# Layer 0's last output projection: first chunk started on channel blocks 4 to 7, weights in half tiles, row buffers moved

## The chip, the cores and the metric

The kernel runs on one core of a Trainium2 chip. The metric is the device time in microseconds. Three runs of the kernel before gave 1709.65, 1710.34 and 1711.06 us; the median is 1710.34 us. One further execution was profiled; its own time was 1717.02 us, its span 1715.2 us.

## What is computed

The program is one step of a two-layer decoder trunk, for a prompt of 1024 tokens and 8 single-token samples, laid side by side as 1032 columns. Layer 0 is an even layer:

```
z_a, xbc, dt, glu_in, z_b = split(x @ w_in)
y   = ssd_scan(silu(conv(xbc)), dt)                    # branch a, a state-space scan
y_a = rms_norm_per_half(y * silu(z_a)) * norm_g        # the gating
y_b = silu(layer_norm(conv(glu(glu_in)))) * silu(z_b)  # branch b, a convolution branch
out = concat(y_a, y_b) @ w_out
x1  = layer_norm(ALPHA * x + out)
```

Layer 1 is sparse attention over x1. The change is in the last step of layer 0: the half of `@ w_out` that belongs to y_a.

## The kernel before, in words

Channels lie on the 128 partitions, in blocks of 128 (eight blocks make the 1024 channels), and the 1032 columns are worked in three chunks of 344 (`CH`). A float32 product is made of three matmuls of float32r halves: an operand is split into hi (a cast on ACT) and lo (a subtraction on DVE or POOL), and `mm3` (L125) adds hi*hi, hi*lo and lo*hi for each of eight channel blocks `kt`: 24 matmuls for each output block m and chunk.

The output projection has two parts. `out_b` (L728) projects the b branch block by block: weights by `load_w` into the rotating weight buffers of `wpool` (tags wst, whi, wlo, three each, half tiles of 128x512), the sum ALPHA*x + p evicted by DVE (L737) and stored to the DRAM tensor `dpart` (L738). Between these blocks the program asks for six gatings (L743). `gate(g, t0, n)` (L702) works on four channel blocks and one chunk: it loads z (L707), multiplies (L708), squares on ACT (L709), adds (L711), sums over the channels with one matmul into the PSUM buffer `pm` (L714), takes the rsqrt with two ACT functions, Ln and Exp (L174 and L175), and scales (L718). Its rows come from the pool `gz`, seven buffers of 128x344.

After `out_b` the pools `ssd`, `gz` and `ob` are closed, and the pools `wst0`, `parts0` and `outp0` are opened in the space they leave. `halves` (L754) splits the gated channels into hi and lo (L756, L757): blocks 4 to 7 over all columns first, then blocks 0 to 3 chunk by chunk. The eight weight tiles of the a branch, 128x1024 each, are loaded whole into two buffers (L775), cast on ACT (L776) and subtracted on DVE for even m and on POOL for odd m (L777), into the sixteen buffers `act` that held y_b. Then, for each chunk, the rows of `dpart` are loaded in two parts of four channel blocks (L786, four buffers of 128x4x344), the eight output blocks are made by `mm3` into PSUM (`pp`, two buffers, for even m; `pt`, five buffers, for odd m) and added to the rows (L791). `layer_norm` (L800) sums the rows (L805), takes the mean with two matmuls (L807 and L808; the second one needs block 7), subtracts it (L812), squares (L814), sums the squares (L816 or L818 and L822), takes Ln and Exp, scales (L828), makes the halves for layer 1 (L829, L830), adds the bias on POOL (L831), and stores the rows to DRAM in two parts (L793). Only that store gives a row buffer free for a later chunk.

Engines run their own instructions in order. The order on each engine is set by a planner that walks the program with a timing model: of the instructions that are ready it takes the one that stands first in the program. So head work of the scan, `out_b`, gatings, weight loads and even layer 1's first weights (L105, L142) are interleaved. `tc.issue_after(ins)` puts the instructions of its block behind `ins` on the engine of `ins`, and binds nothing on other engines. Pools on the left side are laid one after the other in the order in which they are opened. A tile that lands on bytes of a closed pool waits for the last use of those bytes.

Of the kernel before, what the change touches and what calls it, by code (L numbers as in the profile page):

```python
# [9 lines left out]
F32 = mybir.dt.float32  # L10
F32R = mybir.dt.float32r
I32 = mybir.dt.int32
AF = mybir.ActivationFunctionType
ALU = mybir.AluOpType
# [4 lines left out]
T = 1032  # L19
NP = 1024  # L20
NS = 8
CH = [(0, 344), (344, 344), (688, 344)]
# [22 lines left out]
GLU_V, GLU_G, XBC, ZA, ZB, OA, OB = 0, 8, 16, 28, 36, 44, 52  # L45
# [39 lines left out]
def psum(k, shape, tag, bufs, dt=F32):  # L85
    return k.t(k.ps, shape, dt, tag, bufs)


def pp(k):
    return psum(k, [128, 344], "pp", 2)  # L90


def pt(k):
    return k.t(k.pb, [128, 512], F32, "pt", 5)


def pm(k):
    return psum(k, [128, 512], "pm", 1)


def load_half(k, src, h, width=512, eng=None):

    nc = k.nc
    st = k.t(k.wpool, [128, width], F32, "wst", 3)
    load = nc.sync.dma_start(st, src.rearrange("p k c -> p (k c)")[:, h * width : (h + 1) * width])  # L105
    hi = k.t(k.wpool, [128, width], F32R, "whi", 3)
    lo = k.t(k.wpool, [128, width], F32R, "wlo", 3)
    nc.scalar.copy(hi, st)  # L108
    (eng or nc.vector).tensor_tensor(lo, st, hi.bitcast(F32), op=ALU.subtract)  # L109
    return (hi, lo), load.ins  # L110


def load_w(k, src, halves=2, width=512, eng=None):

    return [load_half(k, src, h, width, eng)[0] for h in range(halves)]


def wk(w, kt, m=128, halves=2):
    per = 8 // halves
    hi, lo = w[kt // per]  # L120
    o = (kt % per) * m
    return hi[:, o : o + m], lo[:, o : o + m]


def mm3(k, out, w, act, t0, n, m=128, halves=2, start=True, stop=True):  # L125

    nc = k.nc
    for kt in range(8):
        wh, wl = wk(w, kt, m, halves)
        ah, al = act[kt]  # L130
        ah, al = ah[:, t0 : t0 + n], al[:, t0 : t0 + n]
        nc.tensor.matmul(out, wh, ah, start=(start and kt == 0), stop=False)  # L132
        nc.tensor.matmul(out, wh, al, start=False, stop=False)  # L133
        last = nc.tensor.matmul(out, wl, ah, start=False, stop=(stop and kt == 7))  # L134
    return last.ins


# [33 lines left out]
def rstd_chunk(k, out, var):  # L171

    nc = k.nc
    nc.scalar.activation(out, var, AF.Ln, bias=k.epsb, scale=1.0)  # L174
    nc.scalar.activation(out, out, AF.Exp, scale=-0.5)  # L175


def layer0(k):
    nc, A, tc, ctx = k.nc, k.A, k.tc, k.ctx
    c = k.c  # L180
    es = ExitStack()
    r1_es = ExitStack()
    R1 = r1_es.enter_context(k.pool("R1"))
# [36 lines left out]
    first, last = [], None  # L220
    xst_es = ExitStack()
    xst = xst_es.enter_context(k.pool("xst"))
    for kt in range(8):
        hi = k.t(R1, [128, T], F32R, "act", 16)
        lo = k.t(R1, [128, T], F32R, "act", 16)
        full = k.t(xst, [128, T], F32, "xst", 8)
        for h in [h for h in range(2) if kt == (0, 3)[h]]:
            with tc.issue_after(last) if last else ExitStack():
                half, last = load_half(k, A["W"][GLU_G], h)
                first.append(half)  # L230
        with tc.issue_after(last) if last else ExitStack():
            last = nc.sync.dma_start(full, A["xT"][:, kt]).ins
# [19 lines left out]
    def silu(base, i, dest):  # L252

        w = load_w(k, A["W"][base + i])
        for t0, n in CH:
# [16 lines left out]
    def glu(i):  # L272

        with tc.issue_after(last) if i == 1 else ExitStack():
            w = load_w(k, A["W"][GLU_G + i]) if i else first
        sig = big()
# [4 lines left out]
        with tc.issue_after(last) if i < 2 else ExitStack():  # L281
            w = load_w(k, A["W"][GLU_V + i])
        plain = i in DVE_CONV
# [98 lines left out]
    for t0, n in CH:  # L382
        p = pt(k)[:, :n]
# [11 lines left out]
    for t0, n in CH:  # L395
        p = pt(k)[:, :n]
# [36 lines left out]
    def xbc(i, dest):  # L433
        w = load_w(k, A["W"][XBC + i], eng=nc.gpsimd)
        r = big()
        nc.gpsimd.memset(r[:, 0:3], 0.0)
        for t0, n in CH:
            p = pt(k)[:, :n] if 3 < i < 8 and t0 == 688 else pp(k)
            mm = mm3(k, p, w, x, t0, n)
            if t0 == 344:  # L440
                four_pages(mm)
            m = min(n, NP - t0)
            nc.scalar.copy(r[:, 3 + t0 : 3 + t0 + m], p[:, :m])
            if m < n:
                nc.scalar.copy(ss[:, i, 3, :], p[:, m:n])
        nc.gpsimd.tensor_copy(scp[:, i, :], r[:, NP : NP + 3])
        w, b = hcw[:, :48], hcw[:, 48 + i : 49 + i]
        nc.scalar.activation(dest[:, :NP], r[:, 3 : 3 + NP], AF.Identity, bias=b, scale=w[:, i * 4 + 3 : i * 4 + 4])
        for j in range(3):
            nc.vector.scalar_tensor_tensor(  # L450
                dest[:, :NP], r[:, j : j + NP], w[:, i * 4 + j : i * 4 + j + 1], dest[:, :NP], op0=ALU.mult, op1=ALU.add)
        sc = k.t(tmp, [128, 4, 8], F32, "ssc", 1)
        wbc = w[:, i * 4 : i * 4 + 4].unsqueeze(2).broadcast_to((128, 4, 8))
        nc.vector.tensor_tensor(sc, ss[:, i], wbc, op=ALU.mult)
        nc.vector.tensor_reduce(dest[:, NP:T], sc.rearrange("p k b -> p b k"), axis=AX.X, op=ALU.add)
        nc.vector.tensor_scalar(dest[:, NP:T], dest[:, NP:T], b, None, op0=ALU.add)
        nc.scalar.activation(r[:, :T], dest, AF.Tanh)
        if i in POOL_SILU:
            nc.gpsimd.tensor_tensor(r[:, :T], r[:, :T], dest, op=ALU.mult)
            nc.gpsimd.tensor_tensor(dest, dest, r[:, :T], op=ALU.add)  # L460
        else:
            nc.vector.scalar_tensor_tensor(dest, r[:, :T], 1.0, dest, op0=ALU.add, op1=ALU.mult)
# [16 lines left out]
    for t0, n in CH:  # L479
        p = pp(k)  # L480
        mm_stacked(k, p[:32, :], wdt, x, t0, n)
        nc.scalar.activation(dtr[:32, t0 : t0 + n], p[:32, :], AF.Identity, bias=c("dtb")[:32], scale=1.0)
    p = pm(k)
# [28 lines left out]
    p = pm(k)  # L512
# [13 lines left out]
    for hf in range(2):  # L526
        p = pm(k)
# [7 lines left out]
    p = pm(k)  # L535
# [4 lines left out]
    p = pm(k)  # L540
    for hh in range(8):
        for q in range(2):
            h = 2 * hh + q
# [122 lines left out]
    def silu_za(i):  # L666
        w = load_w(k, A["W"][ZA + i], eng=nc.gpsimd)
        for t0, n in CH:
# [32 lines left out]
    def gate(g, t0, n):  # L701
        sl = slice(t0, t0 + n)  # L702
        ob = lambda: k.t(gzp, [128, 344], F32, "gz", 7)
        sm = None
        for i in range(4 * g, 4 * g + 4):
            z = ob()
            nc.sync.dma_start(z, dza[i][:, sl])  # L707
            nc.vector.tensor_tensor(xs[i][:, sl], xs[i][:, sl], z, op=ALU.mult)  # L708
            nc.scalar.activation(z, xs[i][:, sl], AF.Square)  # L709
            if sm is not None:  # L710
                nc.vector.tensor_tensor(z, z, sm, op=ALU.add)  # L711
            sm = z
        p = pm(k)[:, :n]
        nc.tensor.matmul(p, k.ones["o512"], sm, start=True, stop=True)  # L714
        rs = ob()
        rstd_chunk(k, rs, p)
        for i in range(4 * g, 4 * g + 4):
            nc.vector.scalar_tensor_tensor(xs[i][:, sl], xs[i][:, sl], c("ng")[:, i : i + 1], rs, op0=ALU.mult, op1=ALU.mult)  # L718
# [3 lines left out]
    for i, (hi, lo) in enumerate(yb):  # L722
        full = big()[:, :T]
# [15 lines left out]

    for m in range(8):  # L740
        out_b(m)
        if 1 <= m <= 6:
            gate(1 - (m - 1) // 3, *CH[(m - 1) % 3])  # L743
    ssd_es.close()
    ob_es.close()
    wst = es.enter_context(k.pool("wst0"))
    parts = es.enter_context(k.pool("parts0"))
    op = es.enter_context(k.pool("outp0"))


    yh_pool = k.y_es.enter_context(k.pool("yh", side="right"))
    ya = {}
# [14 lines left out]
            halves(i, t0, n)  # L767


    W = []  # L770
    for m in range(8):
        hi = k.t(R1, [128, T], F32R, "act", 16)
        lo = k.t(R1, [128, T], F32R, "act", 16)
        full = k.t(wst, [128, 1024], F32, "wst", 2)
        nc.sync.dma_start(full, A["W"][OA + m].rearrange("p k c -> p (k c)"))  # L775
        nc.scalar.copy(hi[:, :1024], full)  # L776
        (nc.gpsimd if m % 2 else nc.vector).tensor_tensor(lo[:, :1024], full, hi[:, :1024].bitcast(F32), op=ALU.subtract)  # L777
        W.append([(hi[:, :512], lo[:, :512]), (hi[:, 512:1024], lo[:, 512:1024])])
    dx1 = k.t(dram, [8, 128, T], F32, "dx1")
    for t0, n in CH:  # L780
        sl = slice(t0, t0 + n)
        part, prs = [], []
        for h in range(2):
            pr = k.t(parts, [128, 4, 344], F32, "part", 4)
            prs.append(pr)
            nc.sync.dma_start(pr, dpart[4 * h : 4 * h + 4, :, sl].rearrange("m p t -> p m t"))  # L786
            part += [pr[:, m, :] for m in range(4)]
        for m in range(8):
            p = pt(k)[:, :n] if m % 2 else pp(k)
            mm3(k, p, W[m], ya, t0, n)  # L790
            nc.vector.tensor_tensor(part[m], part[m], p, op=ALU.add)  # L791
        layer_norm(k, op, part, n, t0 + n == T, lambda m: [a[:, sl] for a in ya[m]],
                   lambda h: nc.gpsimd.dma_start(dx1[4 * h : 4 * h + 4, :, sl].rearrange("m p t -> p m t"), prs[h]))  # L793
    es.close()
# [949 lines left out]
```

## Time and profile before

| | us |
|---|---|
| median of three runs | 1710.34 (1709.65 to 1711.06) |
| the profiled execution, its own time | 1717.02 |
| its span | 1715.2 |
| PE busy | 1605.0 (94%) |
| DVE busy | 1205.9 (70%) |
| ACT busy | 850.9 (50%) |
| POOL busy | 243.1 (14%) |

Busy time is the time in which an engine had an instruction in work. Matmuls overlap one another in their pipeline, so their starts, not their lengths, tell the rate. "Idle before, releaser" is the time for which an engine stood still ahead of an instruction, and the instruction or transfer that ended it. A granted clock of 1.00 is 2.4 GHz, one of 0.50 is 1.2 GHz.

### The profile page before, as it was taken

The page shows a single profiled execution, that of the slowest core. Times are in us where ns is not written, and L with a number is a line of the kernel's source. Part 1 is how long each engine was busy: PE and PEld are TensorE (multiplying, and loading weights), DVE is VectorE, ACT ScalarE, POOL GpSimd, SP SyncE. Part 2 cuts the span into 40 slices and gives each one's busy share as a digit, 9 for nine tenths or more (in the row PEclk, how much of TensorE's full clock was granted, in tenths as well). Part 3 has the DMA queues.
Part 4 walks back from the last instruction along what each step waited for, and adds up shares of the span by engine and source line. Part 5 has one row for each costly group of instructions (what it writes and reads, how often), then busy time and mean ns, then how long its engine had stood idle before and what let it go on. Part 6 is the DMA issues. An engine that isn't in the chain of part 4 may idle for free.

```text
span 1715.2 us, 28583 instructions
## 1 busy us (share of the span) xinstructions
PE 1605.0 (94%) x10334; PEld 1442.8 (84%) x10334; DVE 1205.9 (70%) x2742; ACT 850.9 (50%) x1886; POOL 243.1 (14%) x280
## 2 busy tenths in 40 slices
PE   7999989989999998997998999889898899999996
PEld 7999989989999987996898999788886576676674
DVE  4798977460557777756565468999999766565663
ACT  5255423552445564535334456576753655555663
POOL 4000000001222243122322200000000311112120
PEclk9999989999999999998999999999999999999998
DMA  6432243354111254433421214332356324543460
GB/s 221 116 111 67 68 112 96 129 193 135 45 38 58 70 183 162 127 114 121 149 69 54 86 46 132 116 110 92 117 154 182 107 47 112 130 108 87 99 142 29
DMA packets 165649, 185.73 MB, mean 108 GB/s; under 512 B 20324, under 2 KB 131260, under 8 KB 165252
## 3 DMA queue, kind: packets, MB, share of 16 engines
q1 hardware_dynamic: 162996, 178.15, 35.1%
q0 software_dynamic: 1216, 4.37, 0.7%
q8 instruction: 81, 1.33, 0.3%
q10 hardware_dynamic: 1296, 1.38, 0.3%
q14 instruction: 60, 0.49, 0.1%
HBM read 131.91 MB, written 54.05 MB: 108 GB/s over the span
## 4 chain that ended last, share of the span: by engine, by line
PE 69%; DVE 19%; issue 3%; DMA 3%; ACT 3%; POOL 2%; SPq 0%; DVEq 0%; ACTq 0%; POOLq 0%
PE pp L132 11%; PE pp L134 11%; PE pp L133 10%; DVE jkd L1203 6%; PE po L1430 5%; PE pv L1378 4%; PE lg L1342 4%; PE tr L1369 4%; PE pt L625 2%; PE pt L353 2%; PE pt L134 2%; PE pt L132 2%; PE pt L133 2%; ACT cft L351 1%; DVE wlo L109 1%
## 5 line engine op out<-in xcount | busy, mean ns | idle before, releaser
L132 PE MATMUL pp<-act,whi 128*128 128x344 f32 x1016 | 331.3, 328 | 15.3 <-ACT act L233 8.1
L134 PE MATMUL pp<-act,wlo 128*128 128x344 f32 x1016 | 332.4, 329 | 10.7 <-DVE wlo L109 10.7
L133 PE MATMUL pp<-act,whi 128*128 128x344 f32 x1016 | 331.9, 327 | 0.8 <-POOL act L726 0.8
L132 PEld LDWEIGHTS pp<-act,whi 128*128 128x128 f32 x1016 | 195.0, 192 | 18.8 <-ACT act L233 8.1
L134 PEld LDWEIGHTS pp<-act,wlo 128*128 128x128 f32 x1016 | 195.7, 193 | 13.0 <-DVE wlo L109 11.5
L133 PEld LDWEIGHTS pp<-act,whi 128*128 128x128 f32 x1016 | 195.3, 192 | 3.3 <-POOL act L726 1.1
L108 ACT CAST whi<-wst 128x512 fp32r<-128x512 f32 x148 | 90.9, 617 | 153.2 <-PE pp L133 72.9
L334 DVE SCALAR_TENSOR_TENSOR uv<-uv,cst,uv 128x1024 f32<-128x1024 f32 x120 | 157.8, 1315 | 2.6
L132 PE MATMUL pp<-yh,whi 128*128 128x344 f32 x408 | 135.9, 333 | 8.8 <-DVE ev L1080 4.8
L134 PE MATMUL pp<-yh,wlo 128*128 128x344 f32 x408 | 134.2, 329 | 1.0 <-DVE wlo L109 1.0
L109 DVE TENSOR_TENSOR wlo<-wst,whi 128x512 fp32r<-128x512 f32 x104 | 71.4, 692 | 89.5 <-ACT whi L108 89.2
L1342 PE MATMUL lg<-w,Q 128*128 128x512 f32 (+3 forms) x384 | 106.5, 383 | 11.8 <-DVE nmx L1343 11.7
L1343 DVE CUSTOM_DVE_ANT_0 P<-lg,w 128x512 f32<-128x512 f32 (+3 forms) x144 | 82.8, 596 | 45.8 <-PE lg L1342 41.6
L1342 PEld LDWEIGHTS lg<-w,Q 128*128 128x128 f32 x384 | 64.3, 196 | 32.7 <-DVE nmx L1343 20.6
L132 PEld LDWEIGHTS pp<-yh,whi 128*128 128x128 f32 x408 | 80.0, 196 | 12.6 <-DVE ev L1080 6.2
L1369 PE MATMUL tr<-cst,P 128*128 128x128 f32 x576 | 85.9, 282 | 3.5 <-DVE yo L1399 2.9
L1369 PEld LDWEIGHTS tr<-cst,P 128*128 128x128 f32 x576 | 66.0, 143 | 25.6 <-issue 16.5
L1347 ACT ACTIVATE P<-P,mx 128x1024 f32<-128x1024 f32 (+3 forms) x64 | 63.3, 990 | 44.0 <-DVE mx L1346 43.3
L1378 PE MATMUL pv<-ph,V 128*64 128x256 f32 (+1 forms) x640 | 82.3, 372 | 1.4 <-DVE ph L1372 0.8
L134 PEld LDWEIGHTS pp<-yh,wlo 128*128 128x128 f32 x408 | 79.7, 195 | 2.8 <-DVE wlo L109 1.8
L109 POOL TENSOR_TENSOR wlo<-wst,whi 128x512 fp32r<-128x512 f32 x44 | 58.1, 1323 | 156.1 <-ACT whi L108 137.1
L351 ACT ACTIVATE cft<-cw,own 128x80 f32<-128x80 f32 x256 | 66.2, 348 | 22.4 <-PE pt L353 12.2
(565 smaller groups left out, 3942.8 us busy)
## 6 DMA issues: line engine op xcount, KB each, us to landing
wst<-in_W SPq DMA_DIRECT2D x148, 256.0 KB, 2.9
Q<-dq SPq DMA_DIRECT2D x64, 256.0 KB, 4.1
dq<-ev SPq DMA_DIRECT2D x48, 172.0 KB, 1.8
q<-in_ck SPq DMA_DIRECT2D x64, 128.0 KB, 2.4
vp<-in_cv SPq DMA_DIRECT2D x64, 128.0 KB, 2.2
xst<-in_xT SPq DMA_DIRECT2D x8, 516.0 KB, 9.5
dzb<-ob SPq DMA_DIRECT2D x24, 172.0 KB, 2.4
uv<-dzb SPq DMA_DIRECT2D x8, 516.0 KB, 4.2
```

What stands on the lines that cost most here:

```text
L108: nc.scalar.copy(hi, st)
L109: (eng or nc.vector).tensor_tensor(lo, st, hi.bitcast(F32), op=ALU.subtract)
L132: nc.tensor.matmul(out, wh, ah, start=(start and kt == 0), stop=False)
L133: nc.tensor.matmul(out, wh, al, start=False, stop=False)
L134: last = nc.tensor.matmul(out, wl, ah, start=False, stop=(stop and kt == 7))
L334: nc.vector.scalar_tensor_tensor(out, x, w[:, j : j + 1], y, op0=ALU.mult, op1=ALU.add)
L351: nc.scalar.activation(wv[:, :, :, ch, :], taps2, AF.Copy, scale=own[:, ch : ch + 1])
L1203: nc.vector.tensor_scalar(jk, col, c, 0.0, op0=op, op1=ALU.add, accum_out=cnt)
L1342: mm = nc.tensor.matmul(lg, Q[:, 4 * a + r, :], KT[g][:, s0 : s0 + m], start=(a == 0), stop=(a == 1))
L1369: nc.tensor.transpose(p[:, a, r * 128 : r * 128 + 128], Ps[r][:, (sb + a) * 128 : (sb + a) * 128 + 128], k.ident)
L1378: nc.tensor.matmul(pv[64 * u : 64 * u + 64, 256 * pr + c0 : 256 * pr + c1], V[:, sb + a, g * 64 : g * 64 + 64], ph[:, a, c0:c1], start=(sb ...
L1430: nc.tensor.matmul(p, a[:, kt, :], W[kt][w][:, sl], start=start and n == 0, stop=stop and n == 2, skip_group_check=True)
```

## The change

The first chunk of the a branch's projection is made in two passes: first channel blocks 4 to 7 for output blocks 0 to 6 (seven sums open in PSUM at once: five `pt`, two `pp`), then channel blocks 0 to 3 for the same outputs, with the addition to the rows after each; output block 7 follows with both passes. The later chunks are made as before. The weights come as half tiles of 128x512 (four channel blocks each) through the three `wst` buffers of `wpool`. The second halves of output blocks 0 and 1 are first loaded by `load_half` into rotating buffers (`first`), and loaded once more at the end for the later chunks. The gatings of blocks 0 to 3 for chunks 1 and 2 now stand after the first three half tiles of the `act` buffers (m = 2, 3, 4), and their ACT instructions follow the last of these casts. The pool `wst0` is gone, `outp0` comes first, a tile `room` of 128x2700 that nothing reads or writes is put behind it, and `parts0` has three buffers instead of four.

```diff
--- before.py
+++ after.py
@@ -122,16 +122,16 @@
     return hi[:, o : o + m], lo[:, o : o + m]
 
 
-def mm3(k, out, w, act, t0, n, m=128, halves=2, start=True, stop=True):
+def mm3(k, out, w, act, t0, n, m=128, halves=2, kts=range(8), start=True, stop=True):
 
     nc = k.nc
-    for kt in range(8):
+    for kt in kts:
         wh, wl = wk(w, kt, m, halves)
         ah, al = act[kt]
         ah, al = ah[:, t0 : t0 + n], al[:, t0 : t0 + n]
-        nc.tensor.matmul(out, wh, ah, start=(start and kt == 0), stop=False)
+        nc.tensor.matmul(out, wh, ah, start=(start and kt == kts[0]), stop=False)
         nc.tensor.matmul(out, wh, al, start=False, stop=False)
-        last = nc.tensor.matmul(out, wl, ah, start=False, stop=(stop and kt == 7))
+        last = nc.tensor.matmul(out, wl, ah, start=False, stop=(stop and kt == kts[-1]))
     return last.ins
 
 
@@ -739,13 +739,36 @@
 
     for m in range(8):
         out_b(m)
-        if 1 <= m <= 6:
+        if 1 <= m <= 4:
             gate(1 - (m - 1) // 3, *CH[(m - 1) % 3])
+
+
+
+
+    first = [load_half(k, A["W"][OA + m], 1, eng=nc.gpsimd)[0] for m in range(2)]
+    W = {m: [None, None] for m in range(8)}
+    place = {}
+
+    def weights(h, ms):
+        for m in ms:
+            if m not in place:
+                place[m] = [k.t(R1, [128, T], F32R, "act", 16) for _ in range(2)]
+            hi, lo = (a[:, h * 512 : h * 512 + 512] for a in place[m])
+            full = k.t(k.wpool, [128, 512], F32, "wst", 3)
+            nc.sync.dma_start(full, A["W"][OA + m].rearrange("p k c -> p (k c)")[:, h * 512 : h * 512 + 512])
+            cast = nc.scalar.copy(hi, full)
+            (nc.gpsimd if m % 2 else nc.vector).tensor_tensor(lo, full, hi.bitcast(F32), op=ALU.subtract)
+            W[m][h] = hi, lo
+        return cast.ins
+
+    with tc.issue_after(weights(1, range(2, 5))):
+        for t0, n in CH[1:]:
+            gate(0, t0, n)
     ssd_es.close()
     ob_es.close()
-    wst = es.enter_context(k.pool("wst0"))
+    op = es.enter_context(k.pool("outp0"))
+    k.t(es.enter_context(k.pool("room")), [128, 2700], F32, "room", 1)
     parts = es.enter_context(k.pool("parts0"))
-    op = es.enter_context(k.pool("outp0"))
 
 
     yh_pool = k.y_es.enter_context(k.pool("yh", side="right"))
@@ -767,28 +790,34 @@
             halves(i, t0, n)
 
 
-    W = []
-    for m in range(8):
-        hi = k.t(R1, [128, T], F32R, "act", 16)
-        lo = k.t(R1, [128, T], F32R, "act", 16)
-        full = k.t(wst, [128, 1024], F32, "wst", 2)
-        nc.sync.dma_start(full, A["W"][OA + m].rearrange("p k c -> p (k c)"))
-        nc.scalar.copy(hi[:, :1024], full)
-        (nc.gpsimd if m % 2 else nc.vector).tensor_tensor(lo[:, :1024], full, hi[:, :1024].bitcast(F32), op=ALU.subtract)
-        W.append([(hi[:, :512], lo[:, :512]), (hi[:, 512:1024], lo[:, 512:1024])])
+    weights(1, range(5, 8))
+    weights(0, range(8))
+    weights(1, range(2))
     dx1 = k.t(dram, [8, 128, T], F32, "dx1")
     for t0, n in CH:
         sl = slice(t0, t0 + n)
         part, prs = [], []
         for h in range(2):
-            pr = k.t(parts, [128, 4, 344], F32, "part", 4)
+            pr = k.t(parts, [128, 4, 344], F32, "part", 3)
             prs.append(pr)
             nc.sync.dma_start(pr, dpart[4 * h : 4 * h + 4, :, sl].rearrange("m p t -> p m t"))
             part += [pr[:, m, :] for m in range(4)]
-        for m in range(8):
-            p = pt(k)[:, :n] if m % 2 else pp(k)
-            mm3(k, p, W[m], ya, t0, n)
-            nc.vector.tensor_tensor(part[m], part[m], p, op=ALU.add)
+        if t0 == 0:
+            ps = []
+            for m in range(8):
+                p = pt(k)[:, :n] if m in (1, 3, 4, 5, 6) else pp(k)
+                mm3(k, p, [None, first[m]] if m < 2 else W[m], ya, t0, n, kts=(4, 5, 6, 7), stop=False)
+                ps.append(p)
+                if m < 6:
+                    continue
+                for j in range(7) if m == 6 else (7,):
+                    mm3(k, ps[j], W[j], ya, t0, n, kts=(0, 1, 2, 3), start=False)
+                    nc.vector.tensor_tensor(part[j], part[j], ps[j], op=ALU.add)
+        else:
+            for m in range(8):
+                p = pt(k)[:, :n] if m % 2 else pp(k)
+                mm3(k, p, W[m], ya, t0, n)
+                nc.vector.tensor_tensor(part[m], part[m], p, op=ALU.add)
         layer_norm(k, op, part, n, t0 + n == T, lambda m: [a[:, sl] for a in ya[m]],
                    lambda h: nc.gpsimd.dma_start(dx1[4 * h : 4 * h + 4, :, sl].rearrange("m p t -> p m t"), prs[h]))
     es.close()
```

## Rows read from the trace of the kernel before

**Rows 1.** The chain that ended last, from the page: shares of the span by engine

```profile
PE 69%; DVE 19%; issue 3%; DMA 3%; ACT 3%; POOL 2%; SPq 0%; DVEq 0%; ACTq 0%; POOLq 0%
```

**Rows 2.** PE by timeline: start, length, line, operation, count [idle before, releaser]

```profile
807.46 1.51 PE L714 MATMUL pm<-gz,o 128*128 128x344 f32 x2 [6.01 <-DVE gz L711]
...
815.07 0.49 PE L132 MATMUL pp<-yh,act 128*128 128x344 f32 x1
815.36 0.49 PE L133 MATMUL pp<-yb,act 128*128 128x344 f32 x1
...
857.04 0.74 PE L808 MATMUL pt<-part,o 128*128 128x344 f32 x2
...
922.60 0.74 PE L808 MATMUL pt<-part,o 128*128 128x344 f32 x2
...
928.96 1.52 PE L816 MATMUL pt<-sq,o 128*128 128x344 f32 x2 [5.62 <-ACT sq L814]
```

**Rows 3.** Groups of instructions from 780 to 860 us: count | busy, mean ns | idle

```profile
L132 PE MATMUL pp<-yh,act 128*128 128x344 f32 x48 | 16.8, 350 | 4.7 <-ACT act L776 3.4 <-DVE part L791 1.4
L134 PE MATMUL pp<-yh,act 128*128 128x344 f32 x48 | 16.6, 346 | 1.3 <-DVE act L777 1.3
...
L134 PE MATMUL pt<-yh,act 128*128 128x344 f32 x32 | 10.4, 326 | 2.2 <-POOL act L777 2.2
...
L776 ACT CAST act<-wst 128x1024 fp32r<-128x1024 f32 x8 | 8.4, 1044 | 15.8 <-DMA wst<-in_W 15.8
```

**Rows 4.** Stretches: length, busy (count) of PE, PEld, DVE, ACT, POOL, clock, DMA, GB/s

```profile
801.00:807.00 6.00, 0.45 (x3) 0.15 (x1) 6.00 (x6) 1.90 (x2) 3.22 (x3) 0.83 0.27 76
...
812.00:819.00 7.00, 5.32 (x18) 4.88 (x19) 6.79 (x13) 5.50 (x11) 5.87 (x2) 0.52 0.44 139
...
842.00:858.00 16.00, 16.00 (x100) 15.60 (x99) 4.57 (x17) 1.05 (x1) 2.60 (x1) 1.00 0.05 19
```

**Rows 5.** DVE by timeline

```profile
800.25 4.16 DVE L757 TENSOR_TENSOR yl<-yb,yh 128x1032 fp32r<-128x1032 f32 x2
...
806.90 0.50 DVE L711 TENSOR_TENSOR gz<-gz,gz 128x344 f32<-128x344 f32 x1
...
830.02 2.04 DVE L718 SCALAR_TENSOR_TENSOR ya<-ya,cst,gz 128x344 f32<-128x344 f32 x4 [0.58 <-ACT gz L175]
...
892.62 0.51 DVE L791 TENSOR_TENSOR part<-part,pp 128x344 f32<-128x344 f32 x1 [5.88 <-DMA part<-dpart]
```

**Rows 6.** ACT by timeline

```profile
811.26 1.03 ACT L776 CAST act<-wst 128x1024 fp32r<-128x1024 f32 x1
```

**Rows 7.** The SP queue by timeline: start, time to the last issue, line, count

```profile
787.80 17.38 SPq L738 DMA_DIRECT2D dpart<-ob  x4
805.23 0.92 SPq L775 DMA_DIRECT2D wst<-in_W  x2
```

**Rows 8.** Half-tile casts and subtractions over the whole span, from the page

```profile
L108 ACT CAST whi<-wst 128x512 fp32r<-128x512 f32 x148 | 90.9, 617 | 153.2 <-PE pp L133 72.9
...
L109 DVE TENSOR_TENSOR wlo<-wst,whi 128x512 fp32r<-128x512 f32 x104 | 71.4, 692 | 89.5 <-ACT whi L108 89.2
...
L109 POOL TENSOR_TENSOR wlo<-wst,whi 128x512 fp32r<-128x512 f32 x44 | 58.1, 1323 | 156.1 <-ACT whi L108 137.1
```

**Rows 9.** DMA issues from 780 to 900 us: count, size, median us to landing

```profile
part<-dpart SPq DMA_DIRECT2D x6, 688.0 KB, 6.2
wst<-in_W SPq DMA_DIRECT2D x8, 512.0 KB, 4.3
...
wst<-in_W SPq DMA_DIRECT2D x3, 256.0 KB, 3.2
```

**Rows 10.** SP's waits at L786, over the whole span: ns min/median/max

```profile
L786 SPq EVENT_SEMAPHORE  x6: 17/595/49197, 830.3 to 886.5; - x6
```

**Rows 11.** The chain of waits from 740 to 960 us, in order of time

```profile
882.09 3.92 DMA dx<-part
886.07 6.44 DMA part<-dpart
```

## The prediction

> **What bounds the kernel now.** The chain that ended last comes first: 69% of the span hangs on PE [rows 1], so time goes where PE stands still or runs slowly. Going along PE's timeline, the hole at this change is where the b branch's projection ends and the a branch's begins. PE idles 6.0 us ahead of a gating's matmul, which starts at 807.46 [rows 2], then 3.4 us for the cast of the first weight tile, 1.3 and 2.2 us for subtractions of weight tiles, and 1.4 us for a PSUM buffer that DVE has not yet emptied [rows 3]. Together that is 14.3 us. The granted clock tells the rest: it is at full rate to about 805 us and at the lower level, 1.2 GHz, from there to about 818.5 (0.83 over 801 to 807, 0.52 over 812 to 819 [rows 4]). There matmuls start 0.29 us apart [rows 2]; at full clock 100 start in 16 us, 0.157 us apart once the two longer sums are allowed for [rows 4]. Some 13 matmuls ran slowly, at 0.13 us each: 1.7 us. The hole is worth **16.0 us**.
>
> Why it is there: DVE makes the lo halves of blocks 4 and 6 from 800.25 to 804.4, those of the first chunk next, and adds the gating's last square only at 806.90 [rows 5]. ACT holds the first weight cast behind that gating's Ln and Exp, until 811.26 [rows 6]. And the first weight loads stand on SP behind four stores of `dpart`, the last of which waits for the last eviction: they go out at 805.23 [rows 7]. Afterwards ACT waits 15.8 us in all for whole weight tiles [rows 3], which have two buffers.
>
> **The change, part by part.** The matmuls of the chunk stay 192; only their order changes.
>
> *Start.* Blocks 4 to 7 need only the early gatings. Their weights for m = 0 and 1 go through `wpool`, whose buffers come free as `out_b` ends, so their loads need not stand behind the last store. What is late next is the data: DVE's lo halves of blocks 4 and 6, done at 804.4 [rows 5], with up to two half-tile subtractions of 0.69 us [rows 8] now ahead of them: 805.8. PE's previous work ends at 807.46 - 6.01 = 801.45 [rows 2]. The hole is 4.35 us, of which about six matmuls of blocks 4 and 5 fill 0.9: **3.5 us** are left. It lies between 2 (no subtraction goes first) and 6.
>
> *Clock.* An idle stretch of 10 us becomes one of a few. In [rows 4] the clock fell only after PE had stood still from 801.45 to about 805. I take no slow matmul: 0, with 1.7 as the other end.
>
> *Gatings of blocks 0 to 3, chunks 1 and 2.* Moved behind three casts of 0.617 us on ACT [rows 8]; their Ln, Exp and table loads follow, and behind these in ACT's queue stand the casts of later half tiles, for which PE waits. Their eight loads on SP, their products on DVE and the PE matmul keep their places in the program. The PE matmul still stands in order, so if DVE's sums are late PE waits there, as in the 6.0 us now [rows 2]. With four matmuls at 0.16 and the waits I take **1 us**, between 0 and 6, near the low end, as 84 matmuls of the first pass (13.2 us) now lie beside that chain.
>
> *Weights.* Eight issues of 512 KB become 18 of 256 KB, two of them loaded twice. SP pays 0.46 us an issue in [rows 7], 8.3 us instead of 3.7, beside other work. ACT casts 18 x 0.617 = 11.1 us [rows 8] instead of 8.4 [rows 3]. Subtractions are 10 on POOL (13.2 us) and 8 on DVE (5.5 us) [rows 8]. None fills its engine; the turnaround matters. A half tile takes 3.2 us to land [rows 9], 0.6 to cast and 0.7 to 1.3 to subtract, with some 0.5 of issue: 5.0 to 5.6 us, over three buffers 1.7 to 1.9 us each. PE eats one in 12 x 0.157 = 1.88 us. The queues in order make this worse; I take 2.2, for ten half tiles not yet there when PE starts: 10 x 0.32 = **3.2 us**, between 0 and 16 (3.5 us each, one load at a time).
>
> *The rows and their buffers.* By the listed sizes `ob` takes 12,744 + 5,504 + 1,936 bytes, so `gz` begins some 20,200 bytes above the base; with 6,880 and 10,800 bytes ahead of them, the rows' three buffers begin at 17,680, 23,184 and 28,688. The first covers two `gz` buffers and the edge of a third, the last only the end of the seventh. So the rows may still wait for a gating. At 830.02 the last gating scales its rows until 832.1 [rows 5]; rows land 6.2 us after issue [rows 9], at 838. PE holds seven sums open and needs the first addition only for m = 7, near 838: I take 0, with 7 us as the other end.
>
> *Three row buffers instead of four.* The second part of chunk 1 now waits for chunk 0's store, and so does the second part of chunk 2 for chunk 1's. SP already stands up to 49.2 us at such a wait [rows 10]; behind it are chunk 2's rows and layer 1's loads. From the mean's second matmul at 857.04 [rows 2] the store has landed at 886.0 [rows 11]: 29 us. Add a row load of 6.2 [rows 9] and 3 us for additions (0.5 each [rows 5]) and sums, and the next mean stands 38 us behind. The first will start near 841.6 (805.8, plus 192 x 0.157 = 30.1, plus 3.2, 1 and 1.5 for the addition). The third then starts by 841.6 + 76 = 918 where it started at 922.60 [rows 2]. The chain is hidden, by 5 us.
>
> **Sum.** 16.0 goes, 3.5 + 1 + 3.2 = 7.7 come back: 8.3 us gained. The profiled execution's 1717.0 would be 1708.7. It stands 6.7 us above the median, so against the runs I forecast 1710.3 - 8.3 = **1702.0 us**. With one term at its far end at a time the gain lies between 3.3 (gatings) and 11.5 (weights); the far ends of weights and rows on the losing side are rivals below. The row chain, with every link long, caps the gain near 5.
>
> **Rivals.** *More is freed.* PE also idles 5.62 us at 928.96, ahead of the third chunk's squares [rows 2]. If the earlier rows clear this too, and the weights keep pace, 14 to 17 us go: 1693 to 1697. Against it: the wait comes after a static order that is planned anew.
>
> *The rows are not clear of the last gating.* If the first buffer waits for that gating's scaling and the scaling slips with its delayed ACT work to 838, the rows land at 844 and PE, with seven sums open, stands for 6 us: the gain shrinks to 1 to 3, 1707 to 1709.5. For it speaks the overlap in bytes, against it that only the last scale row need lie there.
>
> *Slower: half tiles arrive one at a time.* If SP's order lets only one of the three shared buffers be in flight, a half tile takes 3.2 + 0.3 = 3.5 us. PE has four by 806; twelve more take 42 us, and the first mean starts at 806 + 42 + 1.9 + 1.5 = 851.4. That is hardly ahead of 857.04, and now the three row buffers bind: the third mean at 851.4 + 76 = 927.4, 4.8 us late, 1715.1. It decides from 3.1 us a half tile on. Against it: the whole tiles, in two buffers, landed in 4.3 us [rows 9].
> The Trainium skill (DMA: Bandwidth & Descriptors, "Bandwidth") speaks against the change: it wants DMAs batched to 1 MiB or more. Its fit, 2.0 us plus bytes over 436 GB/s, given for the POOL-issued path, would make two half tiles in turn an estimated 5.2 us against 3.2 for a whole one, 2.0 us more for each of eight tiles. By it alone 16 us would be lost, the whole gain. No run here shows that fit.
> The rows put two half tiles in turn at 6.4 us against 4.3, much the same difference; with three buffers in flight the forecast spreads it.
>
> **Chances.** The forecast case (3.5 to 12 us gained) 0.54, more freed 0.12, rows not clear 0.16, slower 0.18. A change below about 0.2% (3.4 us) can't be told from none. So faster 0.66, same 0.16, slower 0.18. The range, 1693 to 1714, takes in the first three and most of the last.
>
> **What the profile after would show.** Right: PE idle around 801 to 806 of 3 to 5 us at full clock, the first matmuls on channel blocks 4 to 7, and the first mean's second matmul near 841. Wrong in a step: a gating matmul with several us of idle; idle ahead of hi or lo weights of more than 5 us in sum; a wait for `dpart` rows before m = 7; a third mean later than 922.6. If PE's idle up to the first mean falls by the forecast and the time does not, the three row buffers took it back, and L791 of chunks 1 and 2 will show the wait for a row load.

## The result, and the profile after

The changed kernel takes 1726.32 us (median of six runs, 1724.45 to 1730.65), the kernel before 1711.13 us on the same chips. The ratio is 1.0090, with a 95% interval of 1.0076 to 1.0104: **slower by some 15 us**, outside the forecast range. The profiled execution of after has a span of 1726.0 us.

PE by timeline in the kernel after, around the first chunk (start, length, line, operation, count [idle before, releaser]):

```profile
800.22 0.43 PE L133 MATMUL pp<-yl,whi 128*128 128x344 f32 x1 [1.42 <-DVE yl L780]
...
805.62 0.65 PE L134 MATMUL pp<-yh,act 128*128 128x344 f32 x1 [2.87 <-DVE act L760]
...
825.25 0.42 PE L134 MATMUL pp<-yh,act 128*128 128x344 f32 x1 [0.71 <-DVE act L760]
...
829.85 0.66 PE L134 MATMUL pt<-yh,act 128*128 128x344 f32 x1 [1.52 <-POOL act L760]
...
847.11 0.66 PE L132 MATMUL pp<-yh,act 128*128 128x344 f32 x1 [8.10 <-DVE part L815]
847.56 0.49 PE L133 MATMUL pp<-yl,act 128*128 128x344 f32 x1
847.85 0.49 PE L134 MATMUL pp<-yh,act 128*128 128x344 f32 x1
...
856.65 0.74 PE L837 MATMUL pt<-part,o 128*128 128x344 f32 x2
...
891.72 0.63 PE L132 MATMUL pp<-yh,act 128*128 128x344 f32 x1 [7.27 <-DVE part L820]
...
901.11 0.74 PE L837 MATMUL pt<-part,o 128*128 128x344 f32 x2
...
933.00 0.62 PE L158 MATMUL pp<-yh,whi 128*128 128x344 f32 x1 [6.33 <-DVE part L820]
...
940.98 0.74 PE L837 MATMUL pt<-part,o 128*128 128x344 f32 x2
...
942.85 0.85 PE L845 MATMUL pt<-sq,o 128*128 128x344 f32 x2 [0.81 <-ACT sq L843]
...
965.82 0.40 PE L158 MATMUL pp<-yh,whi 128*128 128x344 f32 x1 [3.44 <-DVE ev L940]
```

The lines to set beside [rows 2] are the three means, L837 here. They start at 856.65, 901.11 and 940.98; the first and the third were at 857.04 and 922.60 before. On the profile's clock the first mean is 0.4 us early and the two chunks behind it lost 18.8. But this stage begins earlier here: the last matmul of `out_b` starts at 798.32, and at 801.13 in the profile before. Counted from there, the first mean is 2.4 us late. The short waits ahead of it are less than they were: 1.42, 2.87, 0.25, 0.32, 0.71 and 1.52 us, 7.1 in all, in place of 14.3. But three new waits stand behind them: 8.10, 7.27 and 6.33 us, all of them released by DVE's additions to the rows.

DVE by timeline in the kernel after, around these waits:

```profile
838.20 3.71 DVE L718 SCALAR_TENSOR_TENSOR ya<-ya,cst,gz 128x344 f32<-128x344 f32 x4 [1.11 <-ACT gz L175]
...
846.54 0.51 DVE L815 TENSOR_TENSOR part<-part,pp 128x344 f32<-128x344 f32 x1 [1.79 <-DMA part<-dpart]
...
891.06 0.51 DVE L820 TENSOR_TENSOR part<-part,pp 128x344 f32<-128x344 f32 x1 [7.77 <-DMA part<-dpart]
...
898.58 0.51 DVE L820 TENSOR_TENSOR part<-part,pp 128x344 f32<-128x344 f32 x1 [4.21 <-PE pp L134]
...
932.34 0.51 DVE L820 TENSOR_TENSOR part<-part,pp 128x344 f32<-128x344 f32 x1 [5.91 <-DMA part<-dpart]
```

The SP queue by timeline in the kernel after (start, time to the last issue, count):

```profile
805.59 8.98 SPq L758 DMA_DIRECT2D wst<-in_W  x6
...
816.57 17.85 SPq L758 DMA_DIRECT2D wst<-in_W  x8
...
841.94 1.49 SPq L803 DMA_DIRECT2D part<-dpart  x3
...
885.22 42.49 SPq L803 DMA_DIRECT2D part<-dpart  x3
```

Behind all three waits DVE waits for rows of `dpart`. The first row load goes out at 841.94, right as the last gating's scaling ends (838.20 + 3.71 = 841.91). The others go out at 885.22 and, by the last issue, at 927.7. What they wait for is in the chain of waits of the kernel after, from 838 to 945 us in order of time:

```profile
841.94 4.48 DMA part<-dpart
846.54 0.52 DVE part L815
...
881.24 3.93 DMA dx<-part
885.22 5.71 DMA part<-dpart
891.06 0.52 DVE part L820
...
923.49 3.81 DMA dx<-part
927.35 4.87 DMA part<-dpart
932.34 0.52 DVE part L820
```

Each later load starts when the store of the chunk before has landed: with three buffers, the rows' second part has nowhere else to go.

Stretches of the kernel after: length, busy (count) of PE, PEld, DVE, ACT, POOL, granted clock, DMA share, GB/s:

```profile
806.00:814.00 8.00, 8.00 (x43) 8.00 (x43) 2.72 (x5) 3.77 (x8) 2.28 (x2) 0.81 0.42 133
814.00:822.00 8.00, 8.00 (x51) 7.80 (x50) 3.00 (x7) 6.21 (x10) 2.58 (x2) 1.00 0.79 247
...
826.00:833.00 7.00, 5.48 (x20) 5.04 (x20) 1.70 (x3) 0.90 (x2) 5.03 (x4) 0.51 0.40 127
...
839.00:847.00 8.00, 0.01 (x1) 0.00 (x0) 6.21 (x10) 2.52 (x6) 3.81 (x3) 0.76 0.59 190
847.00:851.00 4.00, 3.89 (x16) 3.89 (x17) 3.96 (x10) 0.00 (x0) 0.00 (x0) 0.62 1.06 389
...
891.00:897.00 6.00, 5.29 (x18) 5.32 (x19) 3.24 (x7) 0.00 (x0) 0.00 (x0) 0.50 0.31 109
```

After every long wait, PE runs at the lower level, 1.2 GHz, for some us: the granted clock is 0.62 over 847 to 851 and 0.50 over 891 to 897, and behind the wait of 6.33 us matmuls start 0.29 us apart until 938.6. PE is also slow in stretches around the short waits (0.81, 0.51).

### The profile page after: what moved, and what is told of

Its sections match the earlier page's. It is cut to its first block, busy times and chain, and to the rows that moved or that the text cites. A ratio compares the mean times of both kernels' runs of the same rounds, so it can differ in the third digit from the quotient of the medians.

```text
span 1726.0 us, 28637 instructions
## 1 busy us (share of the span) xinstructions
PE 1604.9 (93%) x10334; PEld 1441.9 (84%) x10334; DVE 1200.6 (70%) x2746; ACT 852.0 (49%) x1896; POOL 245.3 (14%) x286
## 4 chain that ended last, share of the span: by engine, by line
PE 70%; DVE 18%; ACT 3%; issue 3%; DMA 3%; POOL 1%; SPq 0%; DVEq 0%; ACTq 0%; POOLq 0%
PE pp L134 11%; PE pp L132 11%; PE pp L133 11%; DVE jkd L1232 6%; PE po L1459 5%; PE pv L1407 4%; PE lg L1371 4%; PE tr L1398 4%; PE pt L134 2%; PE pt L132 2%; PE pt L133 2%; PE pt L625 2%; PE pt L353 2%; ACT cft L351 1%; PE pp L158 1%
```

## The experiments

Three explanations stood against each other for the 15 us. **A**: the three row buffers make a chain of store, load, additions, mean. **B**: the row buffers lie where the last gating's do, so chunk 0's rows come late. **C**: the order planned anew and the half-tile weights cost it, whatever the buffers. The remaining runs ask what is left over: the binding of the gatings to the casts, the two passes, and the weight buffers.

Each ratio, with its 95% interval, is that of the kernel's runs to the runs of before that were made beside them. The median of before was 1711.13 us beside after, 1709.66 beside e1 to e4, 1711.56 beside e5 to e8 and 1710.92 beside e9 to e12, so a ratio is not one median of this table over another. The later columns are worked out from one trace of each kernel by subtraction: from the start of the last matmul of `out_b` to the first, second and third mean, and from the third mean to the end of the span. They leave out shifts ahead of this stage. The trace of e9 is that of the slowest of its twelve runs, and the trace of e10 that of the fastest of its five.

| kernel | median us | ratio | to mean 1 | to mean 2 | to mean 3 | rest |
|---|---|---|---|---|---|---|
| before | 1711.13 | 1 | 55.9 | 88.1 | 121.5 | 792.6 |
| after | 1726.32 | 1.0090 (1.0076 to 1.0104) | 58.3 | 102.8 | 142.7 | 785.0 |
| e1_four_rows | 1713.91 | 1.0024 (1.0010 to 1.0039) | 59.6 | 91.7 | 124.0 | 792.8 |
| e2_rows_clear | 1713.76 | 1.0031 (1.0015 to 1.0046) | 52.9 | 94.1 | 135.0 | 783.7 |
| e3_clear_four | 1699.14 | 0.9937 (0.9913 to 0.9961) | 52.4 | 84.5 | 117.4 | 784.9 |
| e4_before_three | 1716.65 | 1.0036 (1.0023 to 1.0050) | 54.3 | 98.5 | 138.1 | 780.7 |
| e5_more_weights | 1699.78 | 0.9938 (0.9924 to 0.9953) | 55.6 | 87.7 | 119.8 | 785.5 |
| e6_one_pass | 1702.04 | 0.9950 (0.9935 to 0.9965) | 55.2 | 87.3 | 119.5 | 786.6 |
| e7_before_clear | 1710.33 | 0.9989 (0.9978 to 1.0000) | 55.9 | 88.0 | 121.4 | 792.8 |
| e8_no_issue_after | 1693.34 | 0.9893 (0.9878 to 0.9909) | 48.8 | 81.0 | 113.1 | 783.7 |
| e9_one_pass_free | 1704.89 | 0.9964 (0.9952 to 0.9977) | 55.9 | 88.1 | 120.2 | 788.7 |
| e10_free_more_weights | 1693.80 | 0.9909 (0.9892 to 0.9926) | 45.0 | 77.2 | 109.3 | 781.7 |
| e11_change_free | 1713.64 | 1.0021 (1.0012 to 1.0031) | 47.7 | 90.5 | 131.9 | 784.4 |
| e12_eighth_again | 1693.64 | 0.9910 (0.9894 to 0.9926) | 49.3 | 81.5 | 113.6 | 782.6 |

**e1: after, with a fourth row buffer** (and a smaller `room`).

```diff
-    k.t(es.enter_context(k.pool("room")), [128, 2700], F32, "room", 1)
+    k.t(es.enter_context(k.pool("room")), [128, 2660], F32, "room", 1)
-            pr = k.t(parts, [128, 4, 344], F32, "part", 3)
+            pr = k.t(parts, [128, 4, 344], F32, "part", 4)
```

> The changed kernel with a fourth row buffer; the unread tile shrinks from 2700 to 2660 numbers so that it fits, and the first buffer still lies on the same bytes of the gating pool. Theory A (three row buffers cost the time): the 7.3 us idle ahead of chunk 2's first sums and the 6.3 us idle near 933 go, the three means stand 32 to 36 us apart instead of 44 and 40, and the time falls by 12 to 17 us, to 1709 to 1714. Theory B (the first rows wait for the last gating): the 8.1 us idle ahead of output block 7 stays and, if it is the only cause, the time stays at 1726. Rival C (the order planned anew and the half-tile weights cost it): 1724 to 1728, whatever the buffers.

**e2: after, with the row buffers first in the space, clear of the gatings' rows**, still three.

```diff
-    op = es.enter_context(k.pool("outp0"))
-    k.t(es.enter_context(k.pool("room")), [128, 2700], F32, "room", 1)
     parts = es.enter_context(k.pool("parts0"))
+    op = es.enter_context(k.pool("outp0"))
```

> The changed kernel with its three row buffers laid first, at the base of the freed space, where none of them touches the gating pool; the unread tile is gone. Theory B: the 8.1 us idle ahead of output block 7 goes, the first mean's second matmul comes at 844 to 848 instead of 856.7, and the chain of three buffers, still 40 to 44 us a link, carries that on: 1715 to 1718. Theory A alone: 1726. Rival C: 1726.

**e3: both** (A, B and C at the base, D behind `outp0`).

```diff
-    op = es.enter_context(k.pool("outp0"))
-    k.t(es.enter_context(k.pool("room")), [128, 2700], F32, "room", 1)
     parts = es.enter_context(k.pool("parts0"))
+    op = es.enter_context(k.pool("outp0"))
+    parts2 = es.enter_context(k.pool("parts2"))
...
-            pr = k.t(parts, [128, 4, 344], F32, "part", 3)
+            tag = "ABCDAB"[2 * (t0 // 344) + h]
+            pr = k.t(parts2 if tag == "D" else parts, [128, 4, 344], F32, "part" + tag, 1)
```

> Both at once: the first chunk's two row buffers and the third at the base, clear of the gating pool, and a fourth buffer above them. If A and B are the two causes, the first mean comes near 846, the third near 912, and the time is 1698 to 1704, faster than the kernel before. Rival C: 1720 or more.

PE by timeline in e1:

```profile
843.73 0.65 PE L132 MATMUL pp<-yh,act 128*128 128x344 f32 x1 [9.31 <-DVE part L815]
...
854.76 0.74 PE L837 MATMUL pt<-part,o 128*128 128x344 f32 x2
...
886.90 0.74 PE L837 MATMUL pt<-part,o 128*128 128x344 f32 x2
...
919.19 0.74 PE L837 MATMUL pt<-part,o 128*128 128x344 f32 x2
```

PE by timeline in e2:

```profile
844.34 0.74 PE L836 MATMUL pt<-part,o 128*128 128x344 f32 x2
...
878.26 0.65 PE L132 MATMUL pp<-yh,act 128*128 128x344 f32 x1 [7.25 <-DVE part L819]
...
885.51 0.74 PE L836 MATMUL pt<-part,o 128*128 128x344 f32 x2
...
918.97 0.62 PE L158 MATMUL pp<-yh,whi 128*128 128x344 f32 x1 [6.47 <-DVE part L819]
```

The SP queue by timeline in e2:

```profile
795.23 0.43 SPq L802 DMA_DIRECT2D part<-dpart  x1
...
799.19 0.92 SPq L802 DMA_DIRECT2D part<-dpart  x2
...
871.81 41.76 SPq L802 DMA_DIRECT2D part<-dpart  x3
```

Each cures one wait and leaves the other. With four buffers the means stand 32.1 and 32.3 us apart again, while the first wait is still there, at 9.31 us. With the rows clear, they are loaded from 795.23 on in place of 841.94 and the first wait is gone, while the chain's 7.25 and 6.47 us stay. Both A and B hold. By the ratios, at 1711 us, the chain costs 0.0066 x 1711 = 11 us, the overlap 0.0059 x 1711 = 10 us, and the two 0.0153 x 1711 = 26 us, each of them to some 3 to 5 us; that the two together cost more than their sum is not clear of that. With both away, e3 is faster than before though it keeps the new order and the half tiles, so C falls.

**e4: the kernel before, with three row buffers** (`"part", 4` to `"part", 3`), the chain by itself.

> The kernel before with three row buffers instead of four and nothing else changed. Theory A: the means stand 40 to 44 us apart, the third comes at about 940 instead of 922.6, and the kernel takes 1722 to 1728. The prediction's view (the chain of three is hidden, 38 us a link at most): 1710 to 1716.

PE by timeline in e4:

```profile
882.56 0.65 PE L132 MATMUL pp<-yh,act 128*128 128x344 f32 x1 [6.95 <-DVE part L791]
...
923.49 0.63 PE L158 MATMUL pp<-yh,whi 128*128 128x344 f32 x1 [6.38 <-DVE part L791]
```

The chain appears in the kernel before too, with the same two waits. Its third mean is 138.1 - 121.5 = 16.6 us later, but the rest is 11.9 us shorter, and the runs say 0.36%, 6 us. So the result fell between the two expectations: what three buffers cost at the third mean is partly given back.

**e7: the kernel before, with its four buffers assigned by hand as in e3**, the control for e3.

> The kernel before with its four row buffers given out by hand so that the first chunk gets two that lie clear of the gating pool; nothing else. Its row loads already stood behind the weight loads and no matmul waited for them, so no change: 1706 to 1712, ratio 0.998 to 1.002. Rival (rows alone give the third experiment's gain): 1699 to 1703.

Nothing changes, as expected: the gain of e3 over before doesn't come from naming the buffers.

**e5: e3 with four weight buffers of their own and the rows asked for ahead.**

```diff
-    def weights(h, ms):
+    def weights(h, ms, pool=k.wpool, bufs=3):
...
-            full = k.t(k.wpool, [128, 512], F32, "wst", 3)
+            full = k.t(pool, [128, 512], F32, "wst", bufs)
...
+    wst = es.enter_context(k.pool("wst0"))
     parts = es.enter_context(k.pool("parts0"))
...
-    weights(1, range(5, 8))
-    weights(0, range(8))
-    weights(1, range(2))
...
+    weights(1, range(5, 8), wst, 4)
+    early = [rows(0, 344, h) for h in range(2)]
+    weights(0, range(8), wst, 4)
+    weights(1, range(2), wst, 4)
```

`rows` loads one part of the rows; its lines are left out here.

> The third experiment (first rows clear, four row buffers) with four more half-tile weight buffers, used from output block 5's second half on; the first chunk's rows are asked for ahead of these loads. If the turnaround of three shared weight buffers holds PE in the first chunk (the waits for casts and subtractions after 805 us, some 6 us in the third experiment), these waits fall to 2 us or less and the time from 1699 to 1693 to 1696. Rival: ACT's and DVE's own queues hold it, and the time stays at 1697 to 1701.

Inconclusive. The new pool pushed the rows' pool up, and the loads of A and B went out only at 823.18 (D at 791.00), so PE waited 3.11 us for an addition. Two things had moved at once; e10 repeats it better.

**e6: e3 without the two passes**, with the loads in the order in which they are then wanted.

```diff
-    weights(1, range(5, 8))
-    weights(0, range(8))
+    weights(0, range(5))
+    for m in range(5, 8):
+        weights(0, [m])
+        weights(1, [m])
     weights(1, range(2))
...
         if t0 == 0:
...
             for m in range(8):
+                p = pt(k)[:, :n] if m % 2 else pp(k)
+                mm3(k, p, [W[m][0], first[m]] if m < 2 else W[m], ya, t0, n)
+                nc.vector.tensor_tensor(part[m], part[m], p, op=ALU.add)
```

> The third experiment without the two passes: chunk 0 is made like the others, block by block over all eight channel blocks, and the half tiles are loaded in the order in which that needs them (first halves ahead). If starting on channel blocks 4 to 7 fills the hole at 800 us, PE now idles 5 to 8 us more before its first full block, and the time is 1704 to 1708. Rival (the gain over the kernel before comes from the rows and the half tiles alone): 1697 to 1701.

PE by timeline in e6:

```profile
804.33 1.52 PE L714 MATMUL pm<-gz,o 128*128 128x344 f32 x2 [13.16 <-DVE gz L711]
```

The hole is back, at 13.16 us ahead of a gating's matmul, yet the time is within 0.13% of e3, with intervals that overlap, and lies between the two ranges expected. So in this surrounding the two passes bring little that can be measured, and the question is why: e3 still pays for something of its own.

**e8: e3 without the binding of the gatings to the casts.** The block stands in the program where it stood.

```diff
-    with tc.issue_after(weights(1, range(2, 5))):
-        for t0, n in CH[1:]:
-            gate(0, t0, n)
+    weights(1, range(2, 5))
+    for t0, n in CH[1:]:
+        gate(0, t0, n)
```

> The third experiment with the gatings of chunks 1 and 2 free of the order on ACT (no binding behind the cast of output block 4). If the binding keeps Ln and Exp out of the casts' way as the prediction priced it (about 1 us), the time is 1698 to 1702. Rival: without it a gating's matmul stands early in PE's order and PE waits 3 to 6 us at it, 1702 to 1706.

**e9: e6, and e11: after itself, with the same edit.**

> The sixth experiment (one pass, half tiles, rows clear, four row buffers) with the gatings free of the order on ACT; against the eighth it lacks only the two passes. If starting on channel blocks 4 to 7 is worth what the prediction's start term said (it took the idle at 800 us from 10 us to 3.5), this is 5 to 8 us slower than the eighth: 1698 to 1702. Rival (once the gatings are early the order of the passes hardly matters): 1693 to 1696.

> The changed kernel with its own row buffers, the gatings free of the order on ACT, and nothing else. If the last gating, delayed behind the casts, is what makes the first rows late, the rows go out 5 to 10 us sooner, the 8.1 us idle ahead of output block 7 shrinks to 0 to 3, and the time falls from 1726 to 1716 to 1720; the chain of three row buffers stays (means 44 and 40 us apart). Rival: the idle stays, 1722 to 1727.

**e10: e8 with four weight buffers of their own**, and the rows in pools of their own (A and B, C, D); **e12: e8 again**, to compare it with.

> The eighth experiment with four more half-tile weight buffers, and the rows in pools of their own so that the first chunk's pool lies wholly clear of the gating pool. If weights still hold PE (2.0 us of waits for casts at 820 in the eighth), 1690 to 1693. Rival: nothing left there, 1692 to 1695. The first rows go out before 815 us, not at 823 as in the fifth experiment, where their pool reached onto the gating's bytes though they did not.

> The eighth experiment once more, beside the two that differ from it in one thing each: 1691 to 1696.

PE by timeline in e8:

```profile
802.39 1.51 PE L714 MATMUL pm<-gz,o 128*128 128x344 f32 x2 [2.64 <-DVE gz L711]
...
814.30 0.84 PE L714 MATMUL pm<-gz,o 128*128 128x344 f32 x2 [2.02 <-DVE gz L711]
```

PE by timeline in e9:

```profile
806.18 1.52 PE L714 MATMUL pm<-gz,o 128*128 128x344 f32 x2 [6.89 <-DVE gz L711]
...
818.08 1.52 PE L714 MATMUL pm<-gz,o 128*128 128x344 f32 x2 [10.38 <-DVE gz L711]
```

DVE by timeline in e11:

```profile
824.24 2.04 DVE L718 SCALAR_TENSOR_TENSOR ya<-ya,cst,gz 128x344 f32<-128x344 f32 x4 [3.43 <-ACT gz L175]
...
830.67 0.51 DVE L815 TENSOR_TENSOR part<-part,pp 128x344 f32<-128x344 f32 x1 [1.59 <-DMA part<-dpart]
```

The binding costs 0.0069 x 1711 = 12 us in the kernel after (e11), and 5 to 8 us where the rows are clear (e12 and e8 against e3). Both are more than expected: e8 came out below both of its ranges, e11 below its own. Up to the first mean, PE waits 11.1 us in all in e3's trace, 6.8 of them for casts and subtractions of weights behind 805 us, and 8.2 us in e8's. In e11 the last gating is scaled by 826.28, the overlapping rows then land before PE has need of them, and the 8.10 us are gone without a change of the buffers; only the chain is left (waits of 7.03 and 6.43 us). With the gatings free the two passes are worth something: e9 is 0.0054 to 0.0071 above e12 and e8, 9 to 12 us, and waits 6.89 + 10.38 us at the gatings where e8 waits 2.64 + 2.02. The two parts of the change hang together: without the two passes, freeing the gatings gains nothing (e9 0.9964, e6 0.9950). More weight buffers bring nothing that the runs can tell (e10 and e12: 0.9909 and 0.9910); the early first mean in e10's trace, at 45.0 us, is that of a single run.

**The best version is e8**, run twice: 0.9893 and 0.9910, some 15 to 18 us under the kernel before. It keeps the two passes and the half tiles, puts the rows first in the space, gives them four buffers, and lets the gatings go free.

## Why the prediction was wrong, point by point

**What held, and what held in number only.** The waits up to the first mean, rows apart, were put at 3.5 + 1 + 3.2 = 7.7 us, and 7.1 were measured. The split was not right. The start was put at 3.5 us, for data; only 1.42 us is a wait for data. The 2.87 us behind it is a wait for a weight: DVE subtracts the lo half for output block 2 from 804.17 to 805.56, behind its lo halves of channel blocks 0 and 2, and takes 1.39 us and not 0.69. So the weights took 2.87 + 0.25 + 0.32 + 0.71 + 1.52 = 5.7 us where 3.2 were forecast, more than the 5 us that the prediction had named as the sign of a wrong step. The gatings' matmuls were put at 1 us; PE waited at none of them. Half tiles did not arrive one at a time: the rival that I took for the slower side did not happen. In the prediction the Trainium skill (DMA: Bandwidth & Descriptors, "Bandwidth") spoke against half tiles, for an estimated 16 us. The traces agree with it on a single tile, and not on the loss: two half tiles in turn would take 2 x 2.9 us to land (the median after) against 4.3 for a whole one, but with three buffers in flight e8 waits only 1.29 + 0.70 us for casts.

The time forecast without the row terms was 1702.0 us, a ratio of 0.9951 to the 1710.34 it was made from, and e3, where both are taken away, gave 0.9937. That is luck in part. The forecast had its 8.3 us in this stage. By e3's trace only 4.1 us are gained at the third mean (117.4 against 121.5), and 7.7 come behind it (784.9 against 792.6). In e8 it is 8.4 at the third mean and 8.9 behind it.

**The step that failed: "The chain is hidden, by 5 us."** The chain was seen, and its links were right but for the last. From the first mean to the landed store I had 29 us, and it took 885.2 - 856.65 = 28.5; the row load took 5.7 of the 6.2 I gave it. But from the rows' landing to the next mean I allowed 3 us "for additions and sums", as if PE's work were done by then. It took 901.11 - 890.93 = 10.2 us in chunk 1, and 940.98 - 932.22 = 8.8 in chunk 2. DVE's additions are what frees PSUM, so while the rows are missing PE can't go on: after them, a whole output block, 24 matmuls 0.287 us apart at the lower clock (6.9 us, to the addition at 898.58), stands between the rows and the mean. In chunk 2 it is a block of 30 matmuls of layer 1 (7.57 us in the chain) that stands ahead of the mean. So the two links take 44.5 and 39.9 us and not 38 each. By these 84.4 us the third mean is on time only if the first starts by 922.60 - 84.4 = 838.2, ahead even of the 841.6 of the forecast. There was no cover, and a rival that rested on this chain alone stood nowhere. The sign that the prediction had named for this case is there: the additions of chunks 1 and 2 (L791 before, L820 after) wait 7.77 and 5.91 us for row loads.

The cover was missing in the prediction's own numbers too. Its first mean, 841.6, stands 15.4 us ahead of the 857.04 before, while its sum gains 8.3. The working counts the chunk's 192 matmuls; from the end of `out_b` to the first mean, 232 start in the profile before and 224 in the profile after, matmuls of chunk 1 among them. The missing 40 are some 40 x 0.157 = 6 us. No trace has so early a mean: 841.6 is 40.5 us behind `out_b`'s last matmul, and the earliest measured is 45.0 (e10). With the first mean 8.3 us ahead, at 848.7, even two links of 38 us end at 924.7, 2.1 us late. And where the prediction says that the chain caps the gain near 5, its sum still takes 8.3.

**The second step: the rows at "0, with 7 us as the other end".** It took 8.10 us, by the mechanism of the rival "The rows are not clear of the last gating", which had 0.16. There the scaling slips to 838, the rows land at 844 and PE stands for 6 us; it began at 838.20, took 3.71 us in place of 2.04 [rows 5], and the rows landed at 846.4. The gating's slip itself was the cost of the binding: its matmul L714 came at 834.33 and its Ln at 835.30, and e11 shows that without the binding it is done at 826.28. I had asked of the moved gatings only whether PE would wait for them, and not what else waited for their end.

**The clock, "no slow matmul", at most 1.7 us.** Ahead of the 8.10 us, 43 matmuls started in 8 us where the next 8 us hold 51 (8 x 0.157 = 1.3 us), and in the 7 us from 826, of which 1.52 were idle, 20 stand where 5.48 / 0.157 = 35 would (15 x 0.157 = 2.4 us): about 3.7 us. After each of the three long waits come slow ones besides.

**How it adds up.** At the third mean, after is 142.7 - 121.5 = 21.2 us later than before, counted from `out_b`'s end; the rest is 7.6 us shorter, together 13.6, where the runs show 15. The 7.6 us come back in three places. Only some 2.0 of them come back near the change: the first matmul on `ki` and `q` in layer 1 (L999 before, L1028 after) starts 57.7 us after the third mean in the kernel before, at 980.31, and 55.7 us after it here, at 996.71. The 5.62 us ahead of the third chunk's squares [rows 2] are 0.81 here, since the chunk is late and PE has layer 1's matmuls to do in that place, but a wait of 3.44 us follows at 965.82 that the kernel before does not have. Another 3.8 us come back between 390 and 465 us after the third mean, and 1.5 in the last 20 us of the span. e3 shows the same three places, with 3.1, 2.9 and 1.5 us. What ties the later two to the change was not tried.

**The range** failed because the two row terms were each kept for a case of its own, one worth 1 to 3 us of gain, the other only behind late weights. Both come from the same edit and came together: with the 10 and 11 us that e2 and e1 show for them the sum is 1723.

**Left open.** How much of the slow clock would go if the short waits at 805 and 829 were taken away, and why e5's loads of A and B wait: by the listed sizes A and B themselves lie clear of the gating's rows and only their pool reaches onto them; in e10, where A and B have a pool of their own, the loads go out at 807.29, but other buffers moved with it.

## What to carry to other kernels

When buffers are taken away, follow the whole loop around one of them (store, load, the first use, and what the waiting engine still has to do after that use) and take the last link from the engine that stands behind it, here a whole block of matmuls for which PSUM had no room. The same gap coming back in every chunk is the sign: the Trainium skill (Perfetto Trace Analysis, "Optimization Strategy") says that a gap repeating on the engine that should be saturated can mean too little room for the next tile, and the traces agree, with 7.27 and 6.33 us at three buffers, and at four none in e1 and 0.92 us in the kernel before. When work is moved later, ask for everything that waits for its end, through memory that is used again too, and not only for its consumers.

## What the hardware showed that was not expected

The three waits of 6 to 8 us cost more than their length: after each of them matmuls start 0.287 us apart, for about nine matmuls (847.56 to 849.86) after the 8.10 us, and for nearly a whole block after the 7.27. And DVE's four scalings of the last gating took 3.71 us in place of 2.04. Within them POOL did a subtraction of 1.64 us (from 838.75), about the difference. In e3 another gating's four scalings took 3.73 us, from 812.90, beside a subtraction of 1.65 us on POOL (from 813.46); in the kernel before, in e8 and at 820.42 in the kernel after, POOL worked on nothing until near their end or later, and they took 2.04 us. That is what the traces show together; no run was made to separate it.
